# Staging of weights in a two-layer hybrid trunk: nine tiles for five, slabs converted by their time under way, modulation slices requested one ahead

## Chip, cores and metric

The kernel runs on one core of a Trainium2 chip. The metric is the device time of one execution in microseconds (us); a kernel's time is the median of its runs.

## What is computed

Two layers follow one another on x of 1024 positions by 1024 channels (float32, batch 1). Cut to what matters here, one layer is:

```python
mod = c_act @ w_mod + b_mod                      # c_act = silu(c), 1024 -> 3072
shift, scale, gate = split(mod, 3)
h = rms_norm(x, pre_gain) * (1 + scale) + shift
proj = h @ w_in                                  # 1024 -> 3088
aq,ak,av,ag, rq,rk,rv,rg, gq,gk,gv,gg, ga = split(proj)
a_out = sliding_window_attention(rotary(aq), rotary(ak), av, sinks) * silu(ag)   # window 128
r_out = rms_norm(retention(rotary(rq), rotary(rk), rv)) * silu(rg)               # chunks of 128
g_out = rms_norm(gated_linear_attention(gq, gk, gv, log_a(ga)), gla_gain) * silu(gg)
y = concat(a_out, r_out, g_out) @ w_out          # 1024 -> 1024
x = x + gate * rms_norm(y, post_gain)
```

The weights of a layer are w_mod (1024 x 3072), w_in (1024 x 3088) and w_out (1024 x 1024), all float32 and all read from device memory.

## The kernel before, in words

**Precision and arenas.** Matrix products run on PE (TensorE). The large ones are done in a reduced float32 form (fp32r) with both operands split into a high and a low part; `accum` runs three passes (high by high, low by high, high by low, PASSES). So each weight has to be *converted* before its use: the high part is a rounding copy and the low part the difference. The converted weights lie in `arena0`/`arena1`, in seven places (PLACES), each of which holds one *unit* of 256 columns (UNITS: `gg`, `rg`, `rq`, ... `kv`, `aq0`, ... `o0` to `o3`). PLACE says which unit lies where, and a place is written again only when PE has read its former unit.

**Staging.** `stage()` hands out a tile of 128 partitions x 512 float32 (256 KB, 2 KB a partition) with the tag `st`, of which there are BST = 5. A unit arrives as four *slabs* of one such tile (`load`, L509: `issue` requests a slab, `conv` converts it). The high part is written at L147 (ACT, `whi1` to `whi3`) or L149 (DVE, `whi0`), the low part at L535 (DVE, `wlo0` to `wlo2`; POOL, `wlo3`). The tile is free for the next transfer when its low part is written. The same tiles hold the slices of w_mod (L360), the row of the post gain (L377), the slabs of the last layer's combinations (below) and, in the output tail, the last product (L1343).

**Order of the work.** PE's instructions run in the order in which the program emits them. The program keeps a clock of its own while it emits (`clk`, advanced by an assumed cost of each matmul), and a list of *jobs*: Python generators that emit the work of the other engines and yield how many of these planner microseconds later they go on (the table L: `ld1`, `mod2`, ...). `pump`, called between groups of matmuls, steps the jobs that are due. So a job's yields decide where in the program its instructions stand; on the other engines the tile scheduler then orders them further. Each engine takes its instructions in order. SP issues nearly all transfers (EN: "S"), in one row, and it waits at a request until the tile that it fills is free.

**The loader** (L475) is such a job. `request` appends a slab to `queue`; the loader takes one slab in 1.2 planner us (`ld1`), requests its transfer and puts it on `flying`. Before that it converts the oldest slabs until no more than LAG + 1 = 3 are under way with the new one. When the queue is empty it converts the rest, one per 1.2 (`ld2`). `drain` (L490) does the same at once.

**Modulation.** `mod_third` (L343) computes a third of `c_act @ w_mod`. For each half of 512 columns it goes over eight slices k: request one slice (256 KB), multiply it by `c_act` and add it to `acc` on DVE (L363, L365), then yield `mod2` = 4.0. The sums over partitions are done by PE at the half's end.

**The last layer's w_out.** The last layer's output projection uses weight blocks and combinations of them (W00, W10, W11, T1 to T4). `sw_first` (L576) requests single slabs through the loader, T1 in pairs; `sw_second` (L596) takes four slabs for each of four k, forms T2, T3 and T4 from them on DVE (L572, L574, L602, L567) and ACT, outside the loader. The output tail that follows works on DVE and ACT (L1335, L1339, L1343).

Of the kernel before, what the change touches and what calls it, by code (L numbers as in the profile page):

```python
# [23 lines left out]
KT = D // P  # L24
# [67 lines left out]
def trunk(ctx: ExitStack, tc: tile.TileContext, ins, cst, out):  # L92
    nc = tc.nc
# [13 lines left out]
    def nm(s):  # L107
        uid[0] += 1
        return f"{s}_{uid[0]}"
# [7 lines left out]
    def stage():  # L117
        return gp.tile([P, 512], F32, tag="st", name=nm("st"), bufs=BST)
# [7 lines left out]
    def aux(dt=F32):  # L126
        return ps.tile([P, 512], dt, tag="aux", name=nm("aux"), bufs=8 - MMB)

    def f(ap):
        return ap.bitcast(F32)  # L130
# [11 lines left out]
    def eng(k):  # L142
        return G if EN[k] == "G" else V
# [7 lines left out]
    def dma(k, dst, src):  # L151
        {"S": nc.sync, "A": A, "P": G}[EN[k]].dma_start(dst, src)
# [5 lines left out]
    clk = [0.0]  # L158
# [3 lines left out]
    def mult(dst, lhsT, rhs, start, stop, cost=None):  # L162
        T.matmul(dst, lhsT, rhs, start=start, stop=stop)  # L163
        if cost is not None:
            clk[0] += cost
            return
        n = 1
        for d in rhs.shape[1:]:
            n *= d
        c = n / 2400.0  # L170
        if rhs.dtype == F32R:
            c = max(c, 0.107 if lhsT.shape[-1] > 64 else 0.055)
        else:
            c = max(4 * c, 0.21 if n > 2 else 0.03)
        clk[0] += c
# [5 lines left out]
    def lat(key, l):  # L181

        return L[key + "@1"] if l and key + "@1" in L else L[key]
# [4 lines left out]
    def flag(name, lat=0.0):  # L188
        flags[name] = clk[0] + lat
# [77 lines left out]
    def mod_rows(l, j, eng=nc.sync):  # L267
        rows = t1()[0:16, 0:P]
        eng.dma_start(rows[0:8, :], b_mod[l:l + 1, j * D:(j + 1) * D].rearrange("o (k p) -> (o k) p", p=P))
        eng.dma_start(rows[8:16, :], pre_g[l:l + 1, :].rearrange("o (k p) -> (o k) p", p=P))  # L270
        return rows

    def mod_rows_t(rows, pool=aux):
        pr = pool()
        transp(pr[:, 0:16], rows, ident[0:16, 0:16])
        rc = small(16)
        V.tensor_copy(rc, pr[:, 0:16])
        return rc

    def mod_cols(l, j, hh, pm, rc):  # L280
        res = modc[(l, j)]
        ks = slice(4 * hh, 4 * hh + 4)
        if j == 0:
            V.tensor_tensor(res[:, ks], pm[:, 0:4], rc[:, ks], ALU.add)
        else:
            col = small(4)
            V.tensor_tensor(col, pm[:, 0:4], rc[:, ks], ALU.add)
            V.scalar_tensor_tensor(res[:, ks], col, 1.0, rc[:, 8 + 4 * hh:12 + 4 * hh], ALU.add, ALU.mult)

    def mod_tile(l, j):  # L290
        modc[(l, j)] = cp.tile([P, KT], F32, name=nm(f"mod{j}"), tag=f"mod{j}")
# [51 lines left out]
    def mod_third(l, j):  # L343
        wv = w_mod[l].rearrange("(p k) n -> p k n", k=KT)
        if j < 2:
            mod_tile(l, j)
            rows = mod_rows(l, j)
            yield lat("mod1", l)
            rc = mod_rows_t(rows)
        else:  # L350
            res = cp.tile([P, D], F32, name=nm("modg"), tag="modg")
            modg[l] = res
        for hh in range(2):
            c0 = j * D + 512 * hh
            acc = gp.tile([P, 512], F32, tag="acc", name=nm("acc"), bufs=1)
            if j == 2:
                G.memset(acc, 0.0)
                nc.sync.dma_start(acc[0:1, :], b_mod[l:l + 1, c0:c0 + 512])
            for k in range(KT):
                wt = stage()  # L360
                dma("lwm", wt, wv[:, k, c0:c0 + 512])
                if k == 0 and j < 2:
                    V.tensor_scalar(acc, wt, c_act[:, k:k + 1], None, ALU.mult)  # L363
                else:
                    V.scalar_tensor_tensor(acc, wt, c_act[:, k:k + 1], acc, ALU.mult, ALU.add)  # L365
                yield lat("mod2", l)
            yield lat("mod3", l)
            pm = aux()
            if j < 2:
                for b in range(4):  # L370
                    mult(pm[:, b:b + 1], acc[:, b * P:(b + 1) * P], ones[:, 0:1], True, True)
                mod_cols(l, j, hh, pm, rc)
                if j == 0:
                    flag(("modh", l, hh), lat("mod4", l))
            else:
                mult(pm, allones, acc, True, True)
                gain = stage()  # L377
                nc.sync.dma_start(gain, post_g[l:l + 1, 512 * hh:512 * hh + 512].to_broadcast((P, 512)))
                V.tensor_tensor(res[:, 512 * hh:512 * hh + 512], pm, gain, ALU.mult)
            yield lat("mod5", l)  # L380
        flag(("mod", l, j), lat("mod6", l))

    def mod_all(l, js, after=None):
        if after is not None:
            yield (0.0, after)
        for j in js:
            yield from mod_third(l, j)
# [81 lines left out]
    queue, flying = [], []  # L469

    def convert():
        conv, st = flying.pop(0)
        conv(*st)

    def loader(l):  # L475
        while queue or flying:
            if queue:
                n, issue, conv = queue.pop(0)
                while flying and sum(len(s) for _, s in flying) + n > LAG + 1:
                    convert()  # L480
                flying.append((conv, issue()))
                yield lat("ld1", l)
            else:
                convert()
                yield lat("ld2", l)
        loading[0] = False

    loading = [False]

    def drain():  # L490
        while queue:
            n, issue, conv = queue.pop(0)
            while flying and sum(len(s) for _, s in flying) + n > LAG + 1:
                convert()
            flying.append((conv, issue()))
        while flying:
            convert()

    def request(l, n, issue, conv):
        queue.append((n, issue, conv))  # L500
        if not loading[0]:
            loading[0] = True
            job(loader(l))
# [774 lines left out]
    class Pair:  # L1278
# [10 lines left out]
        def sum(self):  # L1289
            e = self.e  # L1290
            self.a = []
            for c in range(2):
                s = gp.tile([P, NT * P], F32R, tag=f"kT{c}", name=nm("ma"), bufs=1).rearrange(
                    "p (a k q) -> p a k q", a=2, k=4)
                for a in range(2):
                    dma("lmix", f(s[:, a]), mixS[e, :, a, 4 * c:4 * c + 4])
                self.a.append(s)
            a21, a22, a11, a12 = self.p
            eng("ms0").tensor_tensor(a22, a21, a22, ALU.add)
            eng("ms1").tensor_tensor(a21, a11, a21, ALU.subtract)  # L1300
            eng("ms2").tensor_tensor(a11, a22, a11, ALU.subtract)
            eng("ms3").tensor_tensor(a12, a12, a11, ALU.subtract)
            self.sums = a22, a11, a21, a12
# [362 lines left out]
        pump()  # L1666


B2, B1, BS, BST, MMB, SMB = 10, 8, 11, 5, 3, 3
EN = {"shw0": "V", "shw1": "A", "shw2": "A", "shw3": "A", "slw0": "V", "slw1": "G", "slw2": "V", "slw3": "G", "sht2": "A", "sht3": "A", "sht4": "A", "slt2": "V", "slt3": "G", "slt4": "G", "sd": "V", "mh0": "A", "mh1": "A", "mh2": "A", "mh3": "A", "mf": "A", "ms0": "V", "ms1": "V", "ms2": "V", "ms3": "V", "yg0": "V", "yg1": "V", "ml0": "V", "ml1": "V", "ml2": "V", "ml3": "V", "mod0": "A", "mod1": "V", "qst": "S", "smh": "S", "sml": "S", "sm0": "S", "sm1": "S", "lao": "S", "sao": "S", "lmix": "S", "ssg": "S", "lsg": "S", "ssr": "S", "lsr": "S", "lx": "S", "sx": "A", "lw": "S", "lwm": "S", "whi0": "V", "whi1": "A", "whi2": "A", "whi3": "A", "wlo0": "V", "wlo1": "V", "wlo2": "V", "wlo3": "G", "xn0": "V", "xn1": "V", "hlo0": "V", "hlo1": "V", "rot0": "V", "rot1": "V", "rdec": "V", "kslo": "V", "qslo": "V", "vlo": "G", "kT": "A", "qT": "A", "sprev": "A", "pn": "G", "pf0": "A", "aoc": "A", "hng": "V", "mh": "A", "gso": "V", "mg": "V", "mgl": "V", "rT": "A", "rv": "A", "gv": "A", "gk": "A", "ak0": "V", "ak1": "V", "ak2": "V", "ak3": "V", "kd0": "G", "kd1": "G", "kd2": "G", "kx1": "G", "kx2": "G", "kx3": "V", "kx4": "V", "qb": "G", "stx": "V"}  # L1670
L = {"sw1": 0.4, "ld1": 1.2, "ld2": 1.2, "ld1@1": 1.2, "ld2@1": 1.27, "swW00": 0.0, "swT1": 0.0, "swW11": 0.4, "swW10": 0.5, "tt1": 8.0, "tt2": 1.75, "tb1": 24.5, "tb2": 0.75, "pf3": 13.2, "pf1": 6.35, "pf2": 4.16, "mod1": 4.6, "mod2": 4.0, "mod3": 13.29, "mod4": 7.04, "mod5": 3.36, "mod6": 9.04, "pre1": 7.44, "kv1": 3.1, "kv2": 2.11, "aq1": 6.0, "aq7": 6.0, "ag1": 5.44, "aq2": 2.4, "aq6": 5.2, "aq3": 10.21, "aq4": 7.36, "aq5": 3.6, "hn1": 8.93, "hn2": 2.85, "gz1": 11.18, "gz2": 8.13, "gl1": 2.76, "gd3": 15.9, "gc1": 0.62, "gc2": 1.94, "gc3": 1.33, "gc4": 0.87, "gc6": 0.86, "gc5": 1.14, "rc1": 0.8, "rc2": 1.09, "rc3": 5.87, "rc4": 2.51, "fin1": 7.28, "lay1": 1.13, "gc4@1": 0.93, "mod2@1": 4.0, "mod3@1": 15.1, "mod5@1": 3.36, "mod6@1": 4.11, "pre1@1": 7.44, "kv1@1": 2.79, "kv2@1": 5.28, "aq1@1": 4.8, "aq7@1": 5.28, "ag1@1": 6.25, "aq2@1": 0.82, "aq6@1": 6.0, "aq3@1": 10.9, "aq4@1": 4.4, "aq5@1": 5.15, "hn1@1": 8.12, "hn2@1": 2.85, "gz1@1": 15.91, "gz2@1": 10.94, "gl1@1": 4.6, "gd3@1": 15.9, "gc1@1": 0.48, "gc2@1": 1.94, "gc3@1": 1.33, "gc6@1": 0.86, "gc5@1": 1.04, "rc1@1": 0.37, "rc2@1": 0.84, "rc3@1": 1.9, "rc4@1": 2.79, "fin1@1": 4.28, "lay1@1": 1.7}
CHUNK = 7
LAG = 2
VDB = 8
FIN = 1

# [30 lines left out]
```

## Time and profile before

| | |
|---|---|
| median of three runs | 1006.1 us (1002.45, 1006.10, 1006.14) |
| span of the profiled execution | 1008.9 us, 2.8 above the median; it has no time beside its span |
| PE busy | 975.4 us, 97% |
| weight loads into PE (PEld) | 829.5 us, 82% |
| DVE, ACT, POOL busy | 684.5 (68%), 408.8 (41%), 234.4 us (23%) |
| moved by DMA | 148.73 MB, mean 147 GB/s |
| slabs of w_in, w_mod, w_out | 96, 64 and 52 of 256 KB, median 3.1, 3.3 and 3.8 us from request to landing |

How to read the lines that follow: a timeline row gives the start, the duration, the engine, the line of the kernel and the operation, what it writes and reads by the program's names, and in brackets how long the engine stood before it and what released it. A row of waits gives the engine and its instruction, what it waited for, the microseconds in total, how often, and the longest. A row of a stretch (from:to) gives its length and the busy time of PE, weight loads, DVE, ACT and POOL with their counts, then the clock granted to PE (1.00 is full speed), the share of the time in which the DMA engines were busy, and GB/s. SPq is SP's row of DMA requests; a request's bar is the time of the issue, not of the transfer. Rows with a count join instructions of one kind.

### The profile page before, as it was taken

The page shows a single profiled execution, that of the slowest core. Times are in us where ns is not written, and L with a number is a line of the kernel's source. Part 1 is how long each engine was busy: PE and PEld are TensorE (multiplying, and loading weights), DVE is VectorE, ACT ScalarE, POOL GpSimd, SP SyncE. Part 2 cuts the span into 40 slices and gives each one's busy share as a digit, 9 for nine tenths or more (in the row PEclk, how much of TensorE's full clock was granted, in tenths as well). Part 3 has the DMA queues.
Part 4 walks back from the last instruction along what each step waited for, and adds up shares of the span by engine and source line. Part 5 has one row for each costly group of instructions (what it writes and reads, how often), then busy time and mean ns, then how long its engine had stood idle before and what let it go on. Part 6 is the DMA issues. An engine that isn't in the chain of part 4 may idle for free.

```text
span 1008.9 us, 19610 instructions
## 1 busy us (share of the span) xinstructions
PE 975.4 (97%) x7137; PEld 829.5 (82%) x7137; DVE 684.5 (68%) x1680; ACT 408.8 (41%) x1152; POOL 234.4 (23%) x275
## 2 busy tenths in 40 slices
PE   5899999899999999999999999999999999999897
PEld 1499999888998777778889999998899877777785
DVE  3789857757666778564578275785666577566876
ACT  2476311223322656632465232123332256663321
POOL 2310001223320234330112000113332034544100
PEclk8899999999999999999999999999999999999999
DMA  9942513623326355577655251353132434378883
GB/s 293 308 137 76 173 45 100 170 81 96 96 74 199 89 149 163 171 239 244 214 157 173 64 158 32 108 150 100 41 104 85 125 90 130 112 236 249 265 263 140
DMA packets 129836, 148.73 MB, mean 147 GB/s; under 512 B 14046, under 2 KB 94152, under 8 KB 129740
## 3 DMA queue, kind: packets, MB, share of 16 engines
q1 hardware_dynamic: 124044, 137.92, 45.3%
q10 hardware_dynamic: 5696, 9.56, 2.6%
q8 instruction: 56, 0.92, 0.4%
q14 instruction: 40, 0.33, 0.1%
HBM read 109.17 MB, written 36.18 MB: 144 GB/s over the span
## 4 chain that ended last, share of the span: by engine, by line
PE 80%; DVE 8%; DMA 7%; issue 2%; POOL 1%; ACT 1%; SPq 0%; POOLq 0%; DVEq 0%; ACTq 0%
PE mm L163 61%; PE aux L163 14%; PE aux L178 5%; DMA st<-in_w_in_dram 2%; DMA st<-in_w_out_dram 1%; POOL sm L638 1%; DMA xk<-in_x_dram 1%; DMA wm<-in_w_mod_dram 1%; DMA t<-aoS 1%; DVE arena L535 1%; DMA st<-in_w_mod_dram 1%; DMA t<-sgS 1%; DVE t L328 0%; DVE st L572 0%; DMA mixF<-t 0%
## 5 line engine op out<-in xcount | busy, mean ns | idle before, releaser
L163 PE MATMUL mm<-arena 128*128 128x256 f32 (+2 forms) x1824 | 299.2, 318 | 1.8 <-ACT arena L707 1.8
L163 PE MATMUL mm<-arena,arena 128*128 128x256 f32 (+2 forms) x1824 | 300.7, 318 | 0.0
L163 PEld LDWEIGHTS mm<-arena 128*128 128x128 f32 x1824 | 254.6, 191 | 26.5 <-issue 4.1
L163 PEld LDWEIGHTS mm<-arena,arena 128*128 128x128 f32 x1824 | 254.1, 189 | 25.5 <-issue 4.6
L638 POOL TENSOR_TENSOR sm<-sm,mhalf 128x1 f32<-128x1 f32 (+1 forms) x64 | 56.1, 877 | 347.0 <-DVE sm L637 328.6
L163 PE MATMUL mm<-arena,mx 128*128 128x512 f32 (+1 forms) x564 | 132.4, 392 | 2.9 <-ACT kept L1335 2.9
L163 PEld LDWEIGHTS mm<-arena,mx 128*128 128x128 f32 x564 | 103.1, 191 | 27.1 <-ACT kept L1335 3.3
L147 ACT ACTIVATE t<-aux 128x256 f32<-128x256 f32 (+2 forms) x124 | 55.7, 467 | 76.1 <-PE aux L178 64.8
L147 ACT ACTIVATE arena<-st 128x512 fp32r<-128x512 f32 x94 | 56.1, 626 | 59.1 <-DMA st<-in_w_in_dram 21.4
L535 POOL TENSOR_TENSOR arena<-st,arena 128x512 fp32r<-128x512 f32 x31 | 43.2, 1395 | 138.9 <-ACT arena L147 100.9
L926 POOL TENSOR_TENSOR smx<-smx,sm 128x512 f32<-128x512 f32 x32 | 36.1, 1127 | 124.3 <-DVE sm L925 116.1
L535 DVE TENSOR_TENSOR arena<-st,arena 128x512 fp32r<-128x512 f32 x77 | 59.5, 795 | 6.1 <-ACT arena L147 4.1
L922 ACT ACTIVATE smx<-smx,sm 128x129 f32<-128x129 f32 x128 | 49.9, 392 | 28.4 <-DVE sm L919 28.4
L178 PE MATMUL aux<-c_ident,t 128*128 128x128 f32 (+1 forms) x292 | 48.8, 285 | 7.6 <-DVE t L669 7.2
L365 DVE SCALAR_TENSOR_TENSOR acc<-st,c_act,acc 128x512 f32<-128x512 f32 x60 | 45.5, 759 | 12.6 <-DMA st<-in_w_mod_dram 12.1
L178 PEld LDWEIGHTS aux<-c_ident,t 128*128 128x128 f32 (+1 forms) x292 | 35.4, 145 | 15.2 <-DVE t L669 9.0
L701 ACT ACTIVATE t<-aux,mod,mod 128x128 f32<-128x128 f32 x68 | 25.9, 458 | 43.8 <-DVE t L1242 18.2
L970 ACT ACTIVATE t<-aux 128x256 f32<-128x256 f32 x32 | 12.3, 383 | 75.5 <-PE aux L163 63.4
L163 PEld LDWEIGHTS aux<-t,mx 32*128 32x128 f32 (+1 forms) x896 | 39.5, 187 | 3.8 <-issue 2.1
L163 PE MATMUL aux<-t,mx 32*128 32x32 f32 (+1 forms) x896 | 40.7, 273 | 0.0
L917 DVE COPY_PREDICATED smx<-c_curmask,aux 128x256 f32<-128x256 int32 x64 | 25.5, 447 | 18.8 <-ACT smx L147 15.3
L1242 DVE SCALAR_TENSOR_TENSOR t<-t,sm,t 128x512 f32<-128x512 f32 x32 | 24.0, 779 | 18.6 <-DMA t<-in_x_dram 11.9
(220 smaller groups left out, 1384.3 us busy)
## 6 DMA issues: line engine op xcount, KB each, us to landing
st<-in_w_in_dram SPq DMA_DIRECT2D x96, 256.0 KB, 3.1
st<-in_w_mod_dram SPq DMA_DIRECT2D x64, 256.0 KB, 3.3
st<-in_w_out_dram SPq DMA_DIRECT2D x52, 256.0 KB, 3.8
mx<-mixS SPq DMA_DIRECT2D x20, 512.0 KB, 6.2
mixS<-t SPq DMA_DIRECT2D x72, 128.0 KB, 2.3
wm<-in_w_mod_dram SPq DMA_DIRECT2D x12, 512.0 KB, 8.0
t<-in_x_dram SPq DMA_DIRECT2D x24, 256.0 KB, 4.8
t<-tabS SPq DMA_DIRECT2D x16, 256.0 KB, 3.7
```

The costliest lines, as they stand in the source:

```text
L147: A.activation(dst, src, AF.Copy)
L163: T.matmul(dst, lhsT, rhs, start=start, stop=stop)
L178: T.transpose(dst, src, idn)
L365: V.scalar_tensor_tensor(acc, wt, c_act[:, k:k + 1], acc, ALU.mult, ALU.add)
L535: e.tensor_tensor(lo, st, f(hi), ALU.subtract)
L638: G.tensor_tensor(r, r, mhalf[:, :w], ALU.pow)
L701: A.activation(hf[:, ks], at[kt], AF.Identity, scale=gain, bias=shift)
L917: V.copy_predicated(sv, curmask.unsqueeze(1).to_broadcast((P, 2, P)), pv[:, :, n // P - 1, :])
L922: A.activation(sm[:, h, :], sm[:, h, :], AF.Exp, bias=mx[:, h:h + 1], accum_out=sums[:, h:h + 1])
L926: eng("pn").tensor_tensor(sm[:, :, 0:128], sm[:, :, 0:128], rs.unsqueeze(2).to_broadcast((P, 4, P)), ALU.mult)
L970: A.activation(sq, po, AF.Square)
L1242: V.scalar_tensor_tensor(xt[j], yg[j], r, xt[j], ALU.mult, ALU.add)
```

## The change

It does four things. The program is built with `dynamic_dma_scratch_size=1024`, which takes room in SBUF from software-made transfers, and BST is 9 in place of 5. The loader lets up to AHEAD = 5 slabs be under way; it converts the oldest one when it has been under way for LAND = 5.0 planner us (`aged`), or when the next request would make more than five (`begin`). If nothing is due, it yields until the oldest is. And `mod_third` requests slice k + 1 before it uses slice k; in each half the first request is followed by one more yield of `mod2`.

The number of instructions on each engine and of requests on SP is the same in both kernels. In the changed kernel the lines behind L356 have numbers higher by 5, and those behind `drain` by 11.

```diff
@@ mod_third
+            ahead = []
             for k in range(KT):
-                wt = stage()
-                dma("lwm", wt, wv[:, k, c0:c0 + 512])
+                while len(ahead) + k < min(k + 2, KT):
+                    ahead.append(stage())
+                    dma("lwm", ahead[-1], wv[:, k + len(ahead) - 1, c0:c0 + 512])
+                    if len(ahead) == 1:
+                        yield lat("mod2", l)
+                wt = ahead.pop(0)
                 if k == 0 and j < 2:
@@ loader, drain
     def convert():
-        conv, st = flying.pop(0)
+        conv, st, _ = flying.pop(0)
         conv(*st)
+
+    def aged():
+        return flying and clk[0] - flying[0][2] >= LAND
+
+    def begin(n, issue, conv):
+        while flying and sum(len(s) for _, s, _ in flying) + n > AHEAD:
+            convert()
+        flying.append((conv, issue(), clk[0]))
 
     def loader(l):
         while queue or flying:
-            if queue:
-                n, issue, conv = queue.pop(0)
-                while flying and sum(len(s) for _, s in flying) + n > LAG + 1:
+            if queue and sum(len(s) for _, s, _ in flying) + queue[0][0] <= AHEAD:
+                begin(*queue.pop(0))
+                if aged():
                     convert()
-                flying.append((conv, issue()))
                 yield lat("ld1", l)
-            else:
+            elif aged():
                 convert()
                 yield lat("ld2", l)
+            else:
+                yield flying[0][2] + LAND - clk[0] + 0.01
         loading[0] = False
@@ drain
         while queue:
-            n, issue, conv = queue.pop(0)
-            while flying and sum(len(s) for _, s in flying) + n > LAG + 1:
-                convert()
-            flying.append((conv, issue()))
+            begin(*queue.pop(0))
         while flying:
             convert()
@@ constants
-B2, B1, BS, BST, MMB, SMB = 10, 8, 11, 5, 3, 3
+B2, B1, BS, BST, MMB, SMB = 10, 8, 11, 9, 3, 3
-LAG = 2
+AHEAD = 5
+LAND = 5.0
@@ kernel
-    nc = _bacc.Bacc("TRN2", target_bir_lowering=False, num_devices=1)
+    nc = _bacc.Bacc("TRN2", target_bir_lowering=False, num_devices=1, dynamic_dma_scratch_size=1024)
```

## The prediction, made before the changed kernel ran

> **What bounds the kernel now.** I first read the page: busy shares, slices of PE and its clock, the chain that ended last, the queues.
>
> ```profile
> span 1008.9 us, 19610 instructions
> PE 975.4 (97%) x7137; PEld 829.5 (82%) x7137; DVE 684.5 (68%) x1680; ACT 408.8 (41%) x1152; POOL 234.4 (23%) x275
> PE   5899999899999999999999999999999999999897
> PEclk8899999999999999999999999999999999999999
> q1 hardware_dynamic: 124044, 137.92, 45.3%
> q10 hardware_dynamic: 5696, 9.56, 2.6%
> PE 80%; DVE 8%; DMA 7%; issue 2%; POOL 1%; ACT 1%; SPq 0%; POOLq 0%; DVEq 0%; ACTq 0%
> ```
>
> PE is busy 97% of the span, and the change takes no matmul away. So all that staging can give lies in 1008.9 − 975.4 = 33.5 us in which PE stands, plus what a reduced clock costs behind such a stand. The first slice (25.2 us, digit 5) holds 10 to 12.6 us of it: the start, before the first weights, where the order of SP's requests doesn't change. Next I read the waits, those of the engines that convert or sum slabs, of PE, and of SP, which issues nearly all transfers.
>
> ```profile
> ACT arena L147 <- DMA st<-in_w_in_dram: 21.4, 11, 3.8
> DVE acc L365 <- DMA st<-in_w_mod_dram: 12.1, 9, 3.8
> PE mm L163 <- ACT kept L1335: 2.9, 1, 2.9
> SPq L152 <- ACT t L147: 132.1, 44, 16.5
> SPq L152 <- DVE arena L535: 81.9, 37, 10.5
> ```
>
> ACT and DVE stand 33.5 us for slabs that are still under way, and SP 82 us until a conversion gives a tile back. But these engines are busy 41% and 68%, and PE almost never names them. What counts is where such a wait reaches PE. I went through PE's idle gaps in the timeline for those whose cause is a staging slab, and found four.
>
> **A, near 199 us** (timeline of SP, ACT and PE, then three stretches with PE busy, weight loads, DVE, ACT, POOL, clock, DMA share):
>
> ```profile
> 192.30 0.38 SPq L152 DMA_DIRECT2D st<-in_w_in_dram  x1
> 198.19 0.63 ACT L147 ACTIVATE arena<-st 128x512 fp32r<-128x512 f32 x1 [2.87 <-DMA st<-in_w_in_dram]
> 198.72 0.85 ACT L147 ACTIVATE t<-aux 128x256 fp32r<-128x256 f32 x2
> 199.62 1.23 PE L163 MATMUL aux<-t 64*128 64x128 f32 x8 [3.09 <-ACT t L147]
> 200.78 3.78 PE L163 MATMUL mm<-arena,arena 128*128 128x512 f32 x8
> 204.36 0.63 PE L163 MATMUL aux<-stR,t 128*128 128x128 f32 x2
> 196.20:199.60 3.40, 0.34 (x2) 0.00 (x0) 0.42 (x1) 1.39 (x3) 0.71 (x1) 0.89 0.97 314
> 199.60:203.00 3.40, 3.38 (x13) 2.76 (x14) 0.76 (x2) 0.00 (x0) 0.55 (x1) 0.50 0.80 220
> 203.00:206.50 3.50, 3.50 (x18) 3.13 (x17) 0.00 (x0) 0.01 (x1) 0.00 (x0) 0.61 0.16 49
> ```
>
> ACT works in order. It stands 2.87 us for a slab requested at 192.30, while the two evictions behind it, which PE wants, are ready to go. PE stands 3.09 us, and then its clock is at 0.50 and 0.61: eight matmuls took 204.36 − 200.78 = 3.58 us. At full clock (12 in 3.04 us, below) they take 8 × 0.253 = 2.03, so 1.55 of 3.58 us is lost, and over the 3.40 + 3.50 × 0.78 = 6.1 us at half rate (0.61 means 78% of that stretch) some 2.7. A costs 3.09 + 2.7 = **5.8 us**.
>
> **B, near 683 us**:
>
> ```profile
> 679.60 0.63 ACT L147 ACTIVATE arena<-st 128x512 fp32r<-128x512 f32 x1 [3.77 <-DMA st<-in_w_in_dram]
> 680.77 0.72 PE L163 MATMUL aux<-t 64*128 64x128 f32 x8 [1.28 <-ACT t L147]
> 681.41 3.04 PE L163 MATMUL mm<-arena 128*128 128x512 f32 x12
> 685.46 0.46 PE L163 MATMUL aux<-stR,t 128*128 128x128 f32 x2 [1.01 <-DVE stR L1194]
> 686.46 0.43 PE L163 MATMUL aux<-t,t 128*128 128x64 f32 x2 [0.37 <-DVE t L1173]
> 684.50:688.00 3.50, 2.17 (x15) 1.98 (x16) 1.87 (x6) 0.38 (x1) 1.01 (x1) 1.00 0.60 180
> ```
>
> The same form, with no loss of clock (1.00): 1.28 + 1.01 + 0.37 = **2.7 us**.
>
> **C, near 172 us**, a w_mod slab:
>
> ```profile
> 165.96 0.33 SPq L152 DMA_DIRECT2D st<-in_w_mod_dram  x1
> 171.34 0.75 DVE L365 SCALAR_TENSOR_TENSOR acc<-st,c_act,acc 128x512 f32<-128x512 f32 x1 [3.83 <-DMA st<-in_w_mod_dram]
> 172.48 0.71 PE L163 MATMUL aux<-t 64*128 64x128 f32 x6 [0.54 <-DVE t L963]
> 448.52 0.75 DVE L365 SCALAR_TENSOR_TENSOR acc<-st,c_act,acc 128x512 f32<-128x512 f32 x1 [3.22 <-DMA st<-in_w_mod_dram]
> ```
>
> DVE stands 3.83 us, and PE only 0.54 of it; at 448.52, 3.22 us cost PE nothing. So a wait of DVE reaches PE from about 3.3 us on.
>
> **D, near 946 us**, behind the last layer's weight combinations (sw_second, four slabs at a time):
>
> ```profile
> 922.34 4.56 SPq L152 DMA_DIRECT2D st<-in_w_out_dram  x4
> 927.82 0.33 SPq L152 DMA_DIRECT2D st<-in_w_out_dram  x1
> 929.13 1.20 DVE L572 SCALAR_TENSOR_TENSOR st<-st,gnc,st 128x512 f32<-128x512 f32 x1 [1.38 <-DMA st<-in_w_out_dram]
> 933.51 0.68 DVE L1339 TENSOR_TENSOR t<-aux,kept 128x512 f32<-128x512 f32 x1
> 946.33 4.62 PE L163 MATMUL mm<-arena,mx 128*128 128x512 f32 x12 [2.89 <-ACT kept L1335]
> 946.30:949.70 3.40, 3.37 (x8) 2.70 (x9) 3.08 (x8) 0.72 (x2) 0.00 (x0) 0.51 0.72 195
> ```
>
> With five tiles the last slabs are only requested as tiles come back (922 to 928 us). DVE works through them late, so that its first step of the output tail (L1339) starts at 933.51. The tail's chain on DVE and ACT then ends at "kept", and PE waits 2.89 us and loses 3.40 × 0.49 = 1.7 of clock: D = **4.6 us**.
>
> **The change, part by part.**
>
> *Scratch of 1 KB.* It gives room to the four added tiles (2 KB a partition each). The page has hardware queues only (q1, q10), none of GpSimd's making, so it touches no transfer: 0 us.
>
> *Nine tiles, and up to five slabs under way.* No instruction is added or removed on any engine. In the changed order of SP, weight requests stand earlier. At A, the slab on which ACT stands is asked for ahead of six requests that preceded it before, about 10 us of PE work earlier. It has to land by 199.62 − 3.09 − (199.62 − 198.19) = 195.1, three microseconds earlier than it did; the request moves by more. A goes: **−5.8**. What is late next there is nothing that the timeline shows, since the eight matmuls run as soon as ACT's evictions are done. At B the four ACT waits between 667 and 680 are of the same kind, and the requests move by 3 to 10 us: **−2.7**. At D sw_second can ask for two steps at once; its requests stand about 5 us of PE work earlier, but the order of DVE and ACT in the tail is unchanged, and part of DVE's delay is its own work on the sixteen slabs. Between 0 and −4.6 I take half: **−2.3**. ACT's 21.4 us of waits elsewhere have PE busy beside them: 0.
>
> *Conversion by time.* A unit of four slabs, asked for 1.2 us apart, was converted one by one as later requests pushed; now the last slab is converted 3.6 + 5.0 = 8.6 planner microseconds after the first request, in place of about 7.2: 1.4 us later. The tightest conversion that I found is that of the retention's values (DVE, then PE):
>
> ```profile
> 110.59 0.68 DVE L535 TENSOR_TENSOR arena<-st,arena 128x512 fp32r<-128x512 f32 x1
> 113.31 2.20 PE L163 MATMUL mm<-arena,arena 128*128 128x256 f32 x17
> ```
>
> The written half is done at 111.27, and the matmul that first reads it is in the second row, at 114.0: 2.8 us of cover against 1.4, so 0. Without that cover each microsecond late is one of PE.
>
> *Modulation slices one ahead.* 64 slices are asked for one step (4 planner us) earlier, which is 0 where they came in time, and should remove the nine waits of 12.1 us. But the built order tells otherwise: the slabs for a full arena keep most of the nine tiles until it is read, and the slices' requests take the next tile that comes free, close ahead of their use. 15 of the 64 have under 3 us of PE work between request and use, 16 before. So C stays, and its kind arises in three busy stretches (before 185, about 320 and 540 to 570 us). A median landing is 3.3 us by the page. Bounds: 0 each (as at 448.52), or an A each, 5.8. I take C's price, it being the nearest row: 3 × 0.5 = **+1.5**.
>
> *Sum:* −5.8 − 2.7 − 2.3 + 1.5 = −9.3 on the profiled span of 1008.9, so 999.6. That span is 2.8 above the median of 1006.1, so the forecast is 1006.1 − 9.3 = 996.8, say **997**. The bounds of the parts (D −4.6 to 0, slices 0 to +5.8) give 1006.1 − 13.1 = 993 to 1006.1 − 2.7 = 1003.
>
> **A rule of the Trainium skill beside A.** The page "TensorE: Matmul & The Clock Gate", section "Part 1: The HAM clock gate (the "warmup" mystery)", has the clock fall after an idle window of about 3.4 us, in windows that run free of the kernel. Here 3.09 us of standing sufficed (0.50 behind A), 2.89 too (0.51 behind D), and 1.28 didn't (1.00 behind B); so the trace is below the page's figure, but free-running windows would explain that a run can miss it. If A and D stood without that penalty in a typical execution, as the page's window would allow, the sum would lose 2.7 + 0.9 and come to some 1000.5. I take the trace.
>
> **The rivals.**
>
> *R1, it is no more than the noise.* Waits of ACT and DVE move to another instruction, because SP issues in order: a weight slab that waits for a tile holds back reads and stores behind it, and SP stood 132 us for ACT and 82 us for DVE already. For it: DMA share 0.97 at A, where the same bytes must pass whichever comes first. Against it: SP's waits lie mostly where nothing behind is urgent. If A loses only its stand (3.1), B and D stay and the slices cost 1.5: −1.6, so **1004.5**.
>
> *R2, slower by late slices.* Up to five slabs stand ahead of a slice in SP's order and in the queue; DVE, in order, then stands before L365 with PE's operands behind it. At C a stand of 3.83 us cost 0.5. From about 3.3 + 3.1 = 6.4 us on, PE stands 3.1 us and loses the clock too, 5.8 us each as at A. Two such places eat the gain of 10.8; it decides from three on: −10.8 + 3 × 5.8 = +6.6, so **1012.7**; all five would give 1024. For it: fifteen short leads, in busy stretches. Against it: the longest wait of DVE for a slice is 3.8 us in the trace.
> A rule of the Trainium skill speaks for it: "DMA: Bandwidth & Descriptors", section "Queues, rings and completion order", has each DMA engine take a queue's descriptors in ring order, so that a slice behind five slabs would pay for their bytes. A, where the landing took 198.1 − 192.3 at a DMA share of 0.97, agrees.
>
> *R3, it doesn't do what it says.* The added tiles fill with slabs that wait for their arena, so that slices and last-layer slabs find no free tile: A goes, B stays by half, D stays, slices +1.5: −5.8 − 1.4 + 1.5 = −5.7, so **1000.4**. That is still faster by 0.57%.
>
> *R4, later conversions reach PE.* It takes over 2.8 us; a few units by 1 us each, with the gain kept: about **1001**.
>
> **How the numbers follow.** 0.5%, about what a measurement of this kernel can tell from no change, is 5.0 us: faster is below 1001.1, slower above 1011.1. The runs themselves are 3.7 us apart (1002.45 to 1006.14). Forecast 0.45, R3 0.15, R4 0.06, R1 0.18, R2 0.16. Faster: 0.42 of the forecast, 0.10 of R3, 0.03 of R4 and 0.03 of R1, 0.58. Slower: 0.15 of R2 and 0.02 from elsewhere, 0.17. The rest, 0.25, is within. The forecast's own range is 993 to 1003. With some 3 us for the scatter of the runs it begins at 990; it reaches into R2 up to 1011, which leaves 0.17 above and about 0.03 below.
>
> **What would show it.** Right: no gap of PE over 1 us near 199 and 683, the clock at 1.00 from 199 to 206; ACT's waits for w_in slabs well under 21.4 us; L1339 of the tail before 933.51; the waits of DVE for w_mod slices not under 12.1 us, with PE gaps behind some of them. Wrong: a gap over 3 us with a clock of 0.5 behind a slice (R2), PE waiting for arena L535 or L147 (R4), or the same gaps at A and B with a new releaser (R1).

## The result: slower by 0.84%, and the profile after

The changed kernel took 1013.98 us (median of 5 runs, 1011.87 to 1015.76) against 1003.72 us (5 runs, 1002.45 to 1006.14) before: ratio 1.0084, 95% interval 1.0061 to 1.0108 (the quotient of the two medians, 1.0102, lies within it; all ratios below are those on record, each to runs of the kernel before taken along with it). I had forecast 997 us and given "slower" 0.17.

The profiled execution of the changed kernel has a span of 1010.0 us, and its own time is 1011.87, so 1.9 lie outside the span; it is the shortest of the five. The page and the waits that answer to those of before (the changed kernel's lines are 11 higher behind the loader):

```profile
span 1010.0 us, 19584 instructions
PE 973.9 (96%) x7137; PEld 828.3 (82%) x7137; DVE 694.6 (69%) x1680; ACT 405.9 (40%) x1152; POOL 238.2 (24%) x275
PE   5899999999999999999987999999999999998997
```

```profile
ACT arena L147 <- DMA st<-in_w_in_dram: 2.9, 2, 1.7
DVE acc L370 <- DMA st<-in_w_mod_dram: 9.0, 8, 2.2
PE mm L163 <- DVE t L1232: 4.6, 1, 4.6
PE aux L163 <- POOL t L948: 4.1, 4, 2.3
```

ACT's waits for slabs of w_in fell from 21.4 to 2.9 us: the staging does what it was said to do. The gaps that I had counted are gone or small. At A and B (PE's timeline, then two stretches, with the clock third from the end) there is:

```profile
193.49 0.71 PE L163 MATMUL aux<-t 64*128 64x128 f32 x8 [0.58 <-ACT t L147]
680.88 0.77 PE L163 MATMUL aux<-t,t 128*128 128x64 f32 x4 [0.84 <-DVE t L1184]
196.20:199.60 3.40, 3.40 (x25) 3.08 (x24) 1.40 (x5) 0.96 (x3) 0.41 (x1) 1.00 0.56 185
199.60:203.00 3.40, 3.40 (x23) 3.00 (x22) 1.26 (x3) 0.46 (x2) 1.02 (x2) 1.00 0.01 4
```

0.58 us stand where 3.09 did, 0.84 where 2.7 did, and the clock stays at 1.00. But the slices of PE have a new dent, "87" in the 21st and 22nd, about 505 to 555 us: the passage from layer 1 to layer 2. There PE's timeline and the stretches show:

```profile
526.23 0.66 PE L178 MATMUL aux<-c_ident,t 128*128 128x128 f32 x4 [2.54 <-DVE t L714]
526.64 1.44 PE L163 MATMUL mm<-arena,mx 128*128 128x256 f32 x10
527.91 6.42 PE L163 MATMUL mm<-arena,arena 128*128 128x272 f32 x48
538.90 3.43 PE L163 MATMUL mm<-arena,arena 128*128 128x272 f32 x14 [4.57 <-DVE t L1232]
536.50:539.00 2.50, 0.10 (x1) 0.10 (x1) 2.50 (x9) 2.29 (x7) 0.00 (x0) 1.00 0.41 105
539.00:542.50 3.50, 3.50 (x16) 3.50 (x17) 2.72 (x8) 0.00 (x0) 1.79 (x2) 0.51 0.28 79
```

PE stands 2.54 and 4.57 us for DVE, which is busy all of 536.50 to 539.00, and then runs 3.5 us at 0.51. That is 2.54 + 4.57 + 3.5 × 0.49 = 8.8 us. The kernel before has no gap there. What DVE does in the meantime is seen from its group L703 (L714 after), which applies the modulation of layer 2 to the transposed rows of x, six tiles of positions in this window, and from L284, which finishes a half of that layer's shift. First before, then after:

```profile
L284 DVE TENSOR_TENSOR mod<-aux,sm x2: 155/158/161, 430.5 to 490.3; 128x4 f32<-128x4 f32 x2
L703 DVE TENSOR_SCALAR t<-aux,mod,mod x24: 398/402/410, 498.1 to 527.7; 128x128 f32<-128x128 f32 x24
```

```profile
L284 DVE TENSOR_TENSOR mod<-aux,sm x2: 152/157/162, 448.1 to 515.2; 128x4 f32<-128x4 f32 x2
L714 DVE TENSOR_SCALAR t<-aux,mod,mod x24: 395/402/407, 524.8 to 537.4; 128x128 f32<-128x128 f32 x24
```

The second half of layer 2's shift is ready at 515.2 in place of 490.3, and the same 24 operations begin at 524.8, not at 498.1, and crowd into 12.6 us in place of 29.6. They stand in DVE's row ahead of L1232, which empties the accumulator that PE wants next. The end of that row:

```profile
535.85 2.00 DVE L714 TENSOR_SCALAR t<-aux,mod,mod 128x128 f32<-128x128 f32 x6
537.76 0.68 DVE L722 TENSOR_TENSOR arena<-t,arena 128x512 fp32r<-128x512 f32 x1
538.43 0.42 DVE L1232 TENSOR_TENSOR t<-mm,modg 128x256 f32<-128x256 f32 x1
```

**Theory.** The added yield of 4 planner us in each half lengthens a serial job. From the gate of layer 1 over the two other thirds of layer 2 it runs through six halves, 6 × 4 = 24 us, and the flag "modh" of layer 2, for which `pre` waits, comes 25 us late. **Rival:** the deeper row of requests and the bunched conversions hold DVE and SP up at the boundary. A second question is why the 10.8 us that A, B and D were to give are not seen.

### The profile page after: what moved, and what is told of

It reads as the page before. It is cut to its first block, busy times and chain, and to the rows that moved or that the text cites. A ratio compares the mean times of both kernels' runs of the same rounds, so it can differ in the third digit from the quotient of the medians.

```text
span 1010.0 us, 19584 instructions
## 1 busy us (share of the span) xinstructions
PE 973.9 (96%) x7137; PEld 828.3 (82%) x7137; DVE 694.6 (69%) x1680; ACT 405.9 (40%) x1152; POOL 238.2 (24%) x275
## 5 line engine op out<-in xcount | busy, mean ns | idle before, releaser
L546 POOL TENSOR_TENSOR arena<-st,arena 128x512 fp32r<-128x512 f32 x31 | 45.3, 1464 | 127.6 <-ACT arena L147 62.9
L546 DVE TENSOR_TENSOR arena<-st,arena 128x512 fp32r<-128x512 f32 x77 | 65.1, 869 | 2.0 <-PE mm L163 1.3
L163 PEld LDWEIGHTS aux<-kT,mx 64*128 64x128 f32 x384 | 24.7, 185 | 10.9 <-issue 7.5
```

The lines of the kernel that those rows point to most:

```text
L546: e.tensor_tensor(lo, st, f(hi), ALU.subtract)
```

## The experiments

**1. The changed kernel without the added step.**

```diff
-                    if len(ahead) == 1:
-                        yield lat("mod2", l)
```

> The changed kernel without the one added yield of 4 planner us in each half of a modulation third; the slices are still requested one ahead, nine tiles and the timed conversion stay. Theory (the added step lengthens the modulation's chain, six halves by 4 = 24 us, so that layer 2's shift comes at 515 in place of 490 us and the first preparations of layer 2 collide on DVE at the layer boundary): the second L284 back near 490 us, no gap of PE over 1 us between 515 and 545, 998 to 1004 us. Rival (slabs and slices in a deeper row of requests, and conversions in bunches on DVE, delay the boundary): the gaps near 526 and 539 stay, 1011 to 1015 us.

1004.65 us (12 runs), ratio to before 0.9995 (0.9974 to 1.0017); 9.3 us under the changed kernel by the medians, 0.9% by the two ratios. L284, PE's gap at the boundary, and its waits for POOL:

```profile
L284 DVE TENSOR_TENSOR mod<-aux,sm x2: 157/160/163, 423.0 to 483.5; 128x4 f32<-128x4 f32 x2
536.48 2.02 PE L163 MATMUL mm<-arena,arena 128*128 128x272 f32 x14 [1.63 <-DVE t L998]
PE aux L163 <- POOL t L946: 6.5, 4, 3.2
```

The theory holds: with the same tiles, loader and requests one ahead, the loss is gone. One gap of 1.63 us remains near 536, more than the 1 us that I had allowed, and the time is a little above my 998 to 1004. The gap of 1.6 us comes back in runs 4, 5, 8, 9 and 10, and the kernel before has none there: it is a price of the tiles or the loader, not of the step, and I did not follow it to its cause. Between this profile and that of the changed kernel the spans differ by 5.1 us only: the boundary has 7.2 us less of stands and clock, and PE stands 2.5 us longer for POOL near 900 (3.24 against 0.72).

The time is no better than before, and the profile says why. The stands of A to D, 9.2 us in the first profile of before, are gone, and 8.6 us of new ones have come: 6.5 for POOL's select, in four gaps, 0.4 for ACT beside the last of them, and the 1.63. The 4.0 us that still lie between the two spans (1008.9 and 1004.9) are about the half clock behind A and D (4.4 us). The medians don't show them, since that profile of before is one of a long execution (run 7).

**2. The kernel before with the step alone.**

```diff
+            yield lat("mod2", l)
             for k in range(KT):
                 wt = stage()
```

> The kernel before with nothing changed but one added yield of 4 planner us ahead of the slices of each half of a modulation third: five tiles, the old loader, slices requested at their use. Theory: the same gaps of PE (together 7 us and a half clock behind the longer) at the layer boundary, 8 to 11 us above the kernel before. Rival: no more than 2 us above it.

1023.99 us (5 runs), ratio 1.0193 (1.0168 to 1.0218). The step alone costs 20 us, twice what I expected. L284, and PE's gap with the stretch behind it:

```profile
L284 DVE TENSOR_TENSOR mod<-aux,sm x2: 161/162/163, 455.3 to 520.3; 128x4 f32<-128x4 f32 x2
548.47 6.56 PE L163 MATMUL mm<-arena,arena 128*128 128x272 f32 x38 [2.50 <-DVE t L1220]
549.00:552.50 3.50, 3.50 (x19) 3.50 (x19) 2.96 (x7) 1.99 (x8) 1.21 (x2) 0.57 0.85 291
```

The shift comes 30 us late, and the boundary has its gaps again (0.69, 1.38 and 2.50 us, and 3.5 × 0.43 = 1.5 of clock: 6.1 us). The other 14 us lie elsewhere, in gaps of 1 to 3 us near 196, 222, 251, 421 and 701 among others and in the clock behind them (between 0.60 and 0.85 in the 3.4 us that follow or begin there; PE is busy 983.9 us in place of 975.4). I did not follow these to their causes, so why the step costs twice as much with five tiles stays open.

**3. Half the step in the changed kernel** (`0.5 * lat("mod2", l)`).

> The changed kernel with an added step of 2 planner us a half in place of 4: the second L284 comes 12 us later than without it (near 496), not 25. Theory: a loss in proportion would be 4.7 us (1009); if it only counts once the preparations of layer 2 pile up at the boundary, most of it is still there or most of it is gone: at 496 the six tiles have 30 us left for 6 x 2 us on DVE, so I expect 1004 to 1007. Rival (no link to the chain): 1013.

1009.5 us (7 runs), ratio 1.0042 (1.0026 to 1.0059). L284 came at 497.2, and of the two large gaps at the boundary the first is left, 2.06 us; the second is down to 0.85:

```profile
L284 DVE TENSOR_TENSOR mod<-aux,sm x2: 155/158/161, 435.3 to 497.2; 128x4 f32<-128x4 f32 x2
509.87 0.96 PE L178 MATMUL aux<-c_ident,t 128*128 128x128 f32 x4 [2.06 <-DVE t L714]
541.50 2.02 PE L163 MATMUL mm<-arena,arena 128*128 128x272 f32 x14 [0.85 <-DVE t L1000]
```

No step, half and whole: 0.9995, 1.0042 and 1.0084. As far as intervals of about 0.002 to each side can tell, the loss is in proportion, which I had named and then not expected.

**4. The step paid back at the half's end** (`mod3` 13.29 to 9.29 and 15.1 to 11.1, the step kept).

> The changed kernel with the added step of 4 planner us in each half paid back: the step at the half's end (mod3) is 4 shorter in both layers (13.29 to 9.29, 15.1 to 11.1). Every slice is requested one step ahead, the first too, and the chain of the modulation is no longer than before. Theory (only the chain's length costs): as without the step, 1002 to 1007 us, the second L284 near 485. Rival (the requests one step ahead cost by themselves, by what they push back on SP): above 1008. A third possibility: the sum over partitions now comes too early for DVE's last slice, and PE waits for acc.

1007.14 us (12 runs), ratio 1.0026 (1.0008 to 1.0043), L284 at 485.2, no gap over 2 us at the boundary. This is just above the theory's 1007 and below the rival's 1008. The run was taken on the same chip as run 3, also requests the slices ahead, and is 2.4 us faster with the shift 12 us earlier; most of the changed kernel's loss is gone. So the chain's length is what costs, as in run 1. Whether the requests' lead costs something of its own isn't settled: against run 1 (0.9995, with an interval that overlaps) it would be some 3 us. It brought no gain.

**5. Nine tiles and the new loader, old modulation** (`mod_third` as before).

> The changed kernel with the modulation of the kernel before: nine tiles and the timed conversion alone. Theory: no gap at the layer boundary; the gaps A, B, D of the kernel before gone; 997 to 1003 us. Rival (the loader's row of requests or the later conversions cost): 1008 to 1014 us, with the gaps at 526 and 539.

1006.23 us (12 runs), ratio 1.0014 (0.9999 to 1.0028). The loss is gone here too, but the gain that I expected (997 to 1003 us) isn't there.

**6. Nine tiles alone** (`BST` 9 and the scratch in the kernel before).

> The kernel before with nine tiles (and the 1 KB scratch) alone: old loader, old modulation. If the gaps A and B came of too few tiles, they go here, and the time is 2 to 6 us under before, unless the last layer gives it back (six conversions ahead of the last select on POOL): then 1002 to 1006. If they came of the loader's three slabs, A and B stay and the time is that of before, 1004.

1009.24 us (7 runs), ratio 1.0038 (1.0022 to 1.0055): **slower**, outside what I had named. Its waits, PE's gap at the boundary, and POOL's timeline before the last select:

```profile
ACT arena L147 <- DMA st<-in_w_in_dram: 1.9, 2, 1.7
PE aux L163 <- POOL t L937: 5.2, 4, 2.3
537.78 1.97 PE L178 MATMUL aux<-c_ident,t 128*128 128x128 f32 x8 [2.16 <-DVE t L669]
911.23 5.71 POOL L567 TENSOR_TENSOR arena<-st,arena 128x512 fp32r<-128x512 f32 x4 [2.58 <-PE mm L163]
918.81 3.08 POOL L567 TENSOR_TENSOR arena<-st,arena 128x512 fp32r<-128x512 f32 x2 [1.87 <-ACT arena L147]
921.85 1.08 POOL L937 TENSOR_SCALAR_AFFINE_SELECT t<-t 128x512 f32<-128x512 f32 x1
```

More tiles take ACT's waits for slabs away (1.9 us) without any new loader, and bring a wait of PE for POOL's select, 5.2 us in four gaps, that neither the kernel before nor run 2, with five tiles, has. The six conversions ahead of the last select were named beforehand; that they would cost more than A and B give was not. The loader by time adds nothing to the loss that is seen: with it, run 5 is not slower than this one (another chip, 1.0014 against 1.0038, with intervals that overlap).

**7. The kernel before, profiled again.**

> The kernel before, unchanged, profiled a second time. If the profiled execution of before (span 1008.9 us) was an ordinary one, the gaps A (3.1 us and the half clock) and D (2.9 us and the half clock) are there again. If it was long by chance, the span is about 1002 and A or D or their half clock are missing; then the gain forecast for them was never there to be had in the ordinary execution.

1005.72 us (10 runs). The profiled execution took 1008.83 us, the longest of the ten, with a span of 1007.1. PE's timeline at A, B and D, and the stretches behind them:

```profile
199.96 0.71 PE L163 MATMUL aux<-t 64*128 64x128 f32 x8 [3.06 <-ACT t L147]
679.39 0.87 PE L163 MATMUL aux<-t 64*128 64x128 f32 x8 [2.44 <-ACT t L147]
944.63 1.74 PE L163 MATMUL mm<-arena,mx 128*128 128x512 f32 x6 [2.47 <-ACT kept L1335]
199.90:203.30 3.40, 3.34 (x23) 2.86 (x24) 0.76 (x2) 0.01 (x1) 0.60 (x1) 1.00 0.75 190
679.40:682.80 3.40, 3.40 (x14) 2.70 (x15) 2.70 (x8) 1.25 (x3) 2.21 (x2) 0.56 0.52 134
944.60:948.00 3.40, 3.37 (x11) 2.70 (x12) 3.07 (x8) 0.72 (x2) 0.00 (x0) 0.72 0.73 196
```

The gaps recur, the half clock behind A doesn't: the same stand, 3.06 us against 3.09, was followed by 1.00 here and by 0.50 in the first profile. But B is longer here, 2.44 us in place of 1.28, and is followed by 0.56, where the first profile has 1.00. With the clock of the 3.4 us after these stretches (0.94 behind B, 0.78 behind D) A, B and D cost 3.1, 4.1 and 4.2 us, 11.4 together, against 13.1 in the first profile; the spans differ by about as much, 1.8 us.

**8 and 9. Where the tail's gain went.** POOL's timeline before its last select in the kernel before, then in the changed kernel with PE's gap for it:

```profile
911.30 2.71 POOL L567 TENSOR_TENSOR arena<-st,arena 128x512 fp32r<-128x512 f32 x2 [2.54 <-PE mm L163]
916.02 1.30 POOL L567 TENSOR_TENSOR arena<-st,arena 128x512 fp32r<-128x512 f32 x1 [2.01 <-ACT arena L147]
917.29 1.06 POOL L937 TENSOR_SCALAR_AFFINE_SELECT t<-t 128x512 f32<-128x512 f32 x1
```

```profile
914.26 5.71 POOL L578 TENSOR_TENSOR arena<-st,arena 128x512 fp32r<-128x512 f32 x4 [2.55 <-PE mm L163]
921.85 3.09 POOL L578 TENSOR_TENSOR arena<-st,arena 128x512 fp32r<-128x512 f32 x2 [1.87 <-ACT arena L147]
924.89 1.08 POOL L948 TENSOR_SCALAR_AFFINE_SELECT t<-t 128x512 f32<-128x512 f32 x1
926.02 0.65 PE L163 MATMUL aux<-t,vd 128*64 128x256 f32 x4 [2.27 <-POOL t L948]
```

Six conversions of the last layer's combinations stand ahead of the attention's last select. In the kernel before it is three; my explanation is that with five tiles the scheduler had no tile for the others yet. In run 8 I moved four of sw_second's low parts to DVE (`"slt3": "V"`, without the added step), in run 9 all eight (`"slt4": "V"` too).

> The changed kernel without the added step, and with the low parts of T3 (four conversions of sw_second) on DVE in place of POOL. Theory (what was won at the tail is given back since POOL's conversions stand ahead of the attention's last select, L946): three conversions ahead of it in place of six, 3.9 us earlier; the gap of PE for POOL near 919 (2.3 us) goes and the time falls by 2 to 4 us to about 1001. Rival (DVE is the limit there, and gets 4 x 0.69 us more): no change or slower, 1004 to 1008, with the gap given to DVE.

> As the run with T3's low parts on DVE, and T4's as well: POOL has no conversion ahead of the last select. Theory: the rest of the gap for POOL (1.85 us) goes, 1000 to 1003 us. Rival: DVE has eight conversions more (5.5 us) ahead of what the tail needs, and the time rises to 1004 to 1007.

Run 8 took 1002.75 us (12 runs), ratio 0.9977 (0.9964 to 0.999); PE's gap for the last select only fell from 2.28 us (run 1) to 1.85, as one conversion that waits for ACT still stood right ahead of it. Run 9 took 1001.14 us (7 runs), ratio 0.9944 (0.9924 to 0.9965). POOL's and PE's timeline there:

```profile
911.42 3.72 POOL L946 TENSOR_SCALAR_AFFINE_SELECT t<-t 128x512 f32<-128x512 f32 x1 [8.67 <-ACT t L147]
915.19 0.65 PE L163 MATMUL aux<-t,vd 128*64 128x256 f32 x4 [1.27 <-POOL t L946]
```

The time falls as expected; the gap only shrinks to 1.27 us, with no conversion on POOL ahead of it. What is late is the select itself: it lasts 3.72 us, where the median of the 28 selects in that profile is 0.64. DVE runs eight conversions without a break beside it, 4.90 us from 909.75 on; in run 8 POOL's last conversion ahead of the select lasts 3.62 us beside six on DVE. That one slows the other isn't shown, but moving the work to DVE was not free for POOL.

**10. Nine tiles up to the last layer's combinations, five behind** (without the added step).

```diff
+    held = []
+
+    def hold():
+        cap[0] = 3
+        for _ in range(4):
+            x = stage()
+            G.memset(x[:, 0:1], 0.0)
+            held.append(x)
+
+    def release():
+        for x in held:
+            r = small(1)
+            V.tensor_copy(r, x[:, 0:1])
+
     def sw_first(name):
+        if not held:
+            hold()
```

(`cap[0]` replaces AHEAD in the loader, and `release` stands at the end of sw_second.)

> The changed kernel without the added step, and with four of the nine tiles held (a one-column memset, read again after sw_second) from the first request of the last layer's combinations on, and three slabs under way from there; so nine tiles up to there and five behind it, as before. Theory (nine tiles cost 4.8 us in the last stage since conversions run ahead of the attention's own work on POOL and DVE, more than the gap D gives): the gaps near 832, 838, 900 and 920 go, D comes back, and the last stage is that of before; 999 to 1002 us. Rival (the last stage lost by the timed conversion or by chance): the gaps stay, 1003 to 1006.

1001.26 us (8 runs), ratio 0.9961 (0.9937 to 0.9985), 3.4 us under run 1 by the medians. POOL's timeline at the same place, and PE's at D:

```profile
902.06 2.52 POOL L576 TENSOR_TENSOR arena<-st,arena 128x512 fp32r<-128x512 f32 x2 [2.95 <-PE mm L163]
905.92 1.30 POOL L576 TENSOR_TENSOR arena<-st,arena 128x512 fp32r<-128x512 f32 x1 [1.35 <-ACT arena L147]
907.20 1.06 POOL L963 TENSOR_SCALAR_AFFINE_SELECT t<-t 128x512 f32<-128x512 f32 x1
934.71 3.02 PE L163 MATMUL mm<-arena,mx 128*128 128x512 f32 x12 [0.51 <-ACT kept L1361]
```

Three conversions ahead of the select again, and no gap of PE between 889 and 934. D, which I had expected back, is 0.51 us. This profiled execution has a span of 997.4 us, against 1008.9 and 1007.1 of the two of before; it is the shortest of its eight, and theirs are long ones. Runs 9 and 10 both beat the kernel before and the changed one; their intervals overlap.

## Why the prediction was wrong, point by point

- **"Modulation slices one ahead ... +1.5" is the step that failed.** I counted 64 requests and their leads, and not the yield that came with them. Its 4 planner us a half were "one step earlier" in my working; they are one step later for all that follows in that job. Six halves put the shift of layer 2 from 490.3 to 515.2, 24 preparing operations from 29.6 into 12.6 us, and PE behind them: 9.3 us by the medians (run 1 against the changed kernel; at the boundary the profiles show 8.8 against 1.6), in proportion to the step (run 3). The waits for slices that I priced fell from 12.1 to 9.0 us and cost PE nothing that I found. C's gap is gone as well.
- **A and B went as forecast**, to 0.58 and 0.84 us. Nine tiles alone do most of it (run 6: ACT's wait 1.9 us, PE's gap at A 1.20 us, none at B).
- **D went, but I looked for what is late next in the tail only: the second step that failed.** I wrote that the order of DVE and ACT in the tail was unchanged; POOL's was not, and I put it at nothing. Its conversions moved ahead of the last select, and PE stands for it near 920: 2.27 us in the changed kernel, 1.6 to 2.6 in runs 1 and 3 to 6. Run 6 differs from the kernel before by the tiles alone and has the six conversions, and run 10 goes back to three by holding four tiles and two slabs fewer under way; so the number of tiles sets this order. Runs 9 and 10 get back 3.5 and 3.4 us against run 1 (by the medians, on another chip). Not all of that is the last select: in runs 1, 4 and 6 PE also stands 1.6 to 3.2 us near 900, where POOL itself waits for DVE, and in runs 3, 5 and 8 to 10 it doesn't. What held DVE there, and what makes the two gaps of 0.4 to 0.7 us near 832 and 838, I did not follow.
- **The price of A, B and D was that of long executions.** I took the profiled span as 2.8 above the median. In the profiled executions that have both figures (1010.0 and 1011.87; 1007.1 and 1008.83, for two) a time is 1.7 to 2.0 above its span. So the first profile was an execution of about 1010.7 us, 4.6 above the median of its own three runs and 6.6 above 1004.12, the median of 29 runs of before on the chip of runs 1, 2, 5 and 7. The second profile, of an execution 3.1 above the median of its ten, has the same gaps at 11.4 us together in place of 13.1, with the half clock behind B and D in place of A and D. So the gaps are no accident, but the half clock behind any one of them is. What an execution at the median pays for them, no profile shows. (By the granted clock of A's own two rows its loss is 3.40 × 0.50 + 3.50 × 0.39 = 3.1 us, where I took 2.7.)
- **The sentence on the clock.** In the sentence on the Trainium skill I weighed whether A and D stand without the penalty ("TensorE: Matmul & The Clock Gate", section "Part 1: The HAM clock gate (the "warmup" mystery)") and took the trace. By that page of the Trainium skill the windows run free of the kernel; one stand of 3.1 us that was followed by 0.50 and another that was followed by 1.00 agree with this. Its idle window of about 3.4 us doesn't fit the 2.44 us that were followed by 0.56 (run 7).
- **Conversion by time at 0**: right as far as the runs show. With the new loader (run 5, 1.0014) the kernel is not slower than with nine tiles alone (run 6, 1.0038, on another chip).
- **The rivals.** R2 named the side, with late slices and the price of A; no slice did it. Its sign, a gap over 3 us with a clock of 0.5 behind it, came at the boundary (4.57 us, 0.51), but behind L1232 and not behind a slice. R4 named later conversions, not a later shift. The mechanism that decided was in none. Without the step and with the old tail (run 10) the median is 1001.26 us, still 4 above the forecast of 997, though inside its range.

## What to carry to other kernels

In a program whose order comes from a clock of its own, a yield added to a serial job delays everything that waits for the job's end; follow its flags to their readers, before counting the requests that it moves. More buffers don't only spare waits: they let a scheduler place work earlier on engines that take it in order, ahead of something more urgent. And one profiled execution may carry a clock loss where the next one has none; compare its time with the median, and profile twice before pricing a gap.

## What the runs showed of the hardware that I had not expected

A stand of PE of 3.06 to 3.09 us was followed by a clock of 0.50 in one execution of the same kernel and by 1.00 in another; 4.57 us was followed by 0.51. Nor does the length decide: in run 7 2.44 us was followed by 0.56, in run 3 2.06 us near 510 by 0.51, and in run 1 3.24 us near 898 by 1.00 and 2.28 us near 919 by 0.66, each over the next 3.4 us.

A select on POOL that has a median of 0.64 us lasted 3.72 us while DVE ran eight conversions in a row (run 9). Twenty-nine runs of the kernel before on one chip lay between 1001.78 and 1012.65 us.
